# Key blocks share a turning bank, and the planner's prices change, in a two-layer hybrid attention backbone

## The chip, the cores and the metric

The kernel runs on one core of one Trainium2 chip. The metric is the device time of one execution in microseconds; the time before is the median of three runs. A profile is taken of one further execution; its span goes from the first to the last instruction that the profiler records.

The engines are named as in the profile: PE is TensorE, PEld its weight loads, DVE is VectorE, ACT is ScalarE, POOL is GpSimd, and SP is the queue that issues most of the DMAs.

## The reference

Two trunk layers work on 512 latent tokens and 256 context tokens with 1024 features each, in fp32. A layer is:

```python
mod = c_silu @ ada_w + ada_b            # shift, scale, gate; the same for the context from c_ctx
hx = rmsnorm(x, norm_w) * (1 + scale) + shift
px = split_cols(hx @ w_in)              # q, k, v of three mixers and a gate: 4608 columns
ya = global_gqa(...)                    # A: 8 heads, 2 kv heads, all 768 keys, normed q/k, rotary
yb = neighbourhood_attn(...)            # B: 8 heads, 8 x 16 window of keys with a bias, plus 256 context keys
yc = window_gqa(...)                    # C: 8 heads, 2 kv heads, keys within 128, sink logit, plus context keys
ux = concat([ya, yb, yc]) * silu(px[9])
x = x + gate * (ux @ w_out)
```

Context tokens go through the same weights and read only context keys; in the second layer they are needed as keys and values alone. The output is the final RMSNorm of the latent stream.

## The kernel before

**Numbers.** Every fp32 factor is split into a rounded part and a rest (`wh`/`wl`, `hh`/`hl`, `pth`/`ptl`, the two halves of `qt` and `kt`), both in the type fp32r. A projection is three matmuls (high x high, high x low, low x high); the split of weights costs one ACT copy (L242) and one DVE or POOL subtraction (L245) per 128 x 512 chunk.

**Stages.** The first stage (`p0`) loads x, norms it, makes the first modulation and h block by block, and accumulates the first projections (L416) as each block of h arrives. Then for each layer a stage of projections and attention (`p1`) and a stage of the output projection (`p2`, L505). In `p1` a list (`PLAN`) pairs the attention of one pair of heads with the projections of a later pair, so that TensorE has matmuls while DVE and ACT do the softmax. The last pair of heads (mixer C, pair 3) has no projections beside it; it runs beside the reloads of `u` (`uf`, L485) and the first output products.

**Modulation.** `ada` (L210) multiplies the two conditioning vectors (128 x 2, stationary) with 256 columns of `ada_w` in four column groups of the array at once, in exact fp32: eight products a job, in eight jobs of the first stage and eight in layer 0's `p1`. The row sums of the norms are exact products with a column of ones (`n == 2`). The modulation of layer 1 is mostly done as dot products on DVE (L151).

**Softmax and values.** A unit is one head of one mixer. `scores` puts the scores of a 128-query tile in a bank `Sbig`, DVE takes the maximum, ACT the exponential into `P`. `values` then goes over key blocks: for each it turns the 128 x 128 blocks of `P` of those query tiles that see it into a bank `T` of 512 columns (TensorE transposes, L1031; two such banks), `pt_copy` takes the bank out as `pth` (ACT, L778) and `ptl` (DVE, L1024), and `pv` (L1028) multiplies them with the values into `Obig`. Mixer B is `NearUnit` (16 of them in both layers), mixer C `BandUnit` (16), mixer A `GlobalUnit`, the context queries `CtxUnit`. In a `BandUnit` the blocks 4 and 5 (context) are seen by four tiles, 0 and 3 by two, 1 and 2 by three; in a `NearUnit` 4 and 5 by four, the others by two each.

**Rotary of C.** `rope_c` copies the projection to `tA`, swaps the halves of the heads by four DMAs on SP into `tB` (SBUF to SBUF, L958), and multiplies and adds on POOL (L959 to L961). K of C is then split by ACT (L979), POOL (L980) and copied by DVE (L981).

**The order.** The order of the instructions on each engine is not that of the code. `arrange` makes a `Step` of every instruction with a price (`cost`): the time it holds its engine (`busy`) and the time until its result is there (`last`; for a DMA `move`). `Graph` collects which step needs which, and how many buffers each tile has. `Graph.run` plays all engines and their DMAs forward by list scheduling with a rank; `Graph.back` derives a new rank from behind; after six turns the best of the plays, by its own forecast, is fixed as the order of every engine: PE, ACT, DVE, POOL and SP, whose queue holds the DMAs. The engines work in this order on the chip, each waiting for what its next instruction needs. A price thus changes no instruction, only where it stands.

The prices before, in ns: an exact product of 128 columns 108, any other exact product 230; an fp32r product columns/2.4 plus 12 to 13.5; a POOL operation 190 + 2.14 per element; a DMA lands 2550 plus bytes/395 after it starts, one after the other in one pipe whatever its queue and source.

Of the kernel before, what the change touches and what calls it, by code (L numbers as in the profile page):

```python
# [751 lines left out]
def mixers(tc, nc, l, last, p1, ps, const, env):  # L752
# [274 lines left out]
    def mul(*args, **kw):  # L1027
        return nc.tensor.matmul(*args, **kw)  # L1028

    def turn(*args, **kw):  # L1030
        return nc.tensor.transpose(*args, **kw)  # L1031

    def pv(O, v, pt, o, c0, n, first, final):

        for x in range(2):
            a = mul(O if c0 is None else O[:, c0:c0 + n], v, pt[x][:, o:o + n], start=first and x == 0,
                                 stop=final and x == 1, skip_group_check=True)

            if first and x == 0 and "last" in opv:
                after(a, opv["last"])  # L1040
            if final and x == 1:
                opv["last"] = a.ins.name
# [117 lines left out]
    class BandUnit(Unit):  # L1160
# [32 lines left out]

        def values(self):
            O = psO()
            for n, kb in enumerate((4, 5, 0, 1, 2, 3)):
                qs = [i for i in range(4) if kb in self.pos[i]]
                T = psT()
                for j, i in enumerate(qs):
                    o = self.pos[i][kb]  # L1200
                    turn(T[:, j * 128:(j + 1) * 128], self.P[i][:, o:o + 128], ident)
                k = len(qs) * 128
                pt = pt_copy(T, k)
                yield k / 1200
                pv(O, self.v(kb), pt, 0, qs[0] * 128, k, n == 0, n == 5)
                yield k / 1200
            o_out(O, self.OT(), self.h, 0, NT)

    class NearUnit(Unit):
# [36 lines left out]

        def values(self):
            O = psO()
            for n, kb in enumerate((4, 5, 1, 2, 3, 0)):
                qs = [i for i in range(4) if kb in self.PLAN[i][4]]  # L1250
                T = psT()
                for j, i in enumerate(qs):
                    o = self.PLAN[i][4][kb]
                    turn(T[:, j * 128:(j + 1) * 128], self.P[i][:, o:o + 128], ident)
                k = len(qs) * 128
                pt = pt_copy(T, k)
                yield k / 1200
                out = O[:, qs[0] * 128:qs[0] * 128 + k] if kb else O.rearrange("p (t c) -> p t c", t=4)[:, 0:4:3]
                pv(out, self.v(kb), pt, 0, None, k, n == 0, n == 5)
                yield k / 1200  # L1260
            o_out(O, self.OT(), self.h, 0, NT)

# [211 lines left out]
    prev = None  # L1474
# [24 lines left out]
    for pair, items, n_ada in PLAN:  # L1499
# [3 lines left out]
        if pair is not None:  # L1503
            kind, i = pair
            if kind == "B":
                Q, K = made["b", i]
                prev = units("B", i, Q, K, made["v", i // 2][i % 2], lambda i=i: made["g", i // 2][i % 2], bmb)
            else:
                Q, G = made[kind.lower(), i]
                K, V = made[kind.lower() + "kv", 0]  # L1510
                prev = units(kind, i, Q, K, V, G, bmc if kind == "C" else None)
# [6 lines left out]
        t = sum(time[k] for k, i in items)  # L1518
# [6 lines left out]
    prev = units("C", 3, Q, K, V, G, bmc)  # L1525
# [21 lines left out]
            xn1=8, rbl=2)  # L1547
POOLS = ("p0_", "p1_0_", "p2_0_", "p1_1_", "p2_1_")
BANKS = ("pj", "T", "Sbig", "Obig")
TO_PE, TO_OTHER, FIXED, RATE = 400.0, 150.0, 2550.0, 395.0  # L1550
ISSUE = dict(tB=580.0, R5=520.0, R2=520.0, wr=680.0)
WAIT = {"PE": 53.0, "POOL": 78.0, "ACT": 36.0, "DVE": 36.0, "SP": 30.0}
BEHIND = {"ACT": 112.0, "DVE": 85.0, "POOL": 45.0}
# [2 lines left out]
def stem(name):  # L1556
    return name.rsplit("_", 1)[0]
# [9 lines left out]
class Step:  # L1567


    def __init__(self, inst):  # L1570
        self.inst, self.name = inst, inst.name
        self.engine = ENGINES[str(inst.engine).split(".")[-1]]
        self.kind = type(inst).__name__
        self.dma = self.kind == "InstDMACopy"
        self.use = []
        for args, writes in ((inst.ins, 0), (inst.outs, 1)):
            for a in args:
                b = getattr(a, "bass_ap", None)
                if b is not None:
                    self.use.append((b.tensor, writes, tuple((int(p), int(q)) for p, q in a.ap), int(b.offset),  # L1580
                                     str(a.dtype).split(".")[-1]))
        self.cost()

    def cost(self):
        ins = [u for u in self.use if not u[1]]
        outs = [u for u in self.use if u[1]]
        n = max([size(u[2]) for u in ins + outs[:1]] or [0])
        bank = any(stem(u[0].name) in BANKS for u in ins)
        op = str(getattr(self.inst, "op", getattr(self.inst, "func", ""))).split(".")[-1]
        e = self.engine  # L1590
        self.plain, self.turn, self.switch = False, None, 0.0
        if self.dma:
            b = 4 * outs[0][2][0][1] * size(outs[0][2])
            self.busy = ISSUE.get(stem(outs[0][0].name).split("_")[0], 430.0)
            self.move = 3460.0 if stem(outs[0][0].name) == "bc" else b / RATE
        elif e == "PE":
            n = size(ins[0][2])
            exact = ins[0][4] == "float32"
            self.turn = outs[0][0].name if stem(ins[0][0].name) in ("ident", "identr") and n == 128 else None
            self.switch = 5.0 if exact else 86.0  # L1600
            self.busy = (108.0 if n == 128 else 230.0) if exact else n / 2.4 + (13.5 if n > 128 else 12.0)
            self.last = 272.0 if exact else n / 2.4 + 180.0
        else:
            if e == "ACT":
                d = 172.0 + 0.83 * n + (0 if bank else 35)
            elif e == "DVE":
                d = 156.0 + 0.52 * n if self.kind == "InstTensorCopy" and not bank else 152.0 + 1.06 * n
                self.plain = self.kind == "InstTensorTensor" and not bank and n >= 256
            elif op == "pow":
                d = 1000.0  # L1610
            elif self.kind == "InstTensorScalarPtr":
                d = 440.0 + 2.2 * n if n > 8 else 190.0
            else:
                d = 190.0 + 2.14 * n if n > 64 else 150.0
            self.busy = max(d - BEHIND[e], 20.0)
            self.last = d
            if e == "ACT" and op == "Exp" and n > 12:
                self.busy, self.last = d - 16, d + 91
# [18 lines left out]
class Graph:  # L1637
# [76 lines left out]
    def run(self, rank):  # L1714

        steps, n = self.steps, len(self.steps)
# [12 lines left out]
        for t, v in self.order.items():  # L1729
            if self.pool[t] is not None:  # L1730
                stage_left[self.pool[t]] += len(v)
        lanes, pipe = [], 0.0
        prev, done = None, 0

        def push(k):
            heapq.heappush(later[steps[k].engine], (ready[k], rank[k], k))
# [9 lines left out]
        while done < n:  # L1746
            t, e = min((max(free[e], -1.0 if now[e] else later[e][0][0]), e) for e in later if now[e] or later[e])
            free[e] = t = max(t, free[e])
            while later[e] and later[e][0][0] <= t:
                _, r, k = heapq.heappop(later[e])  # L1750
# [7 lines left out]
            r, k = heapq.heappop(now[e])  # L1758
            s = steps[k]
            need, wait = t, None  # L1760
            for name in self.opens[k]:
                tag = self.tag[name]
                p = self.pool[tag]
# [20 lines left out]
                wake(tag, t)  # L1784
            busy = s.busy
            if s.dma:
                pipe = fin = max(t + FIXED, pipe) + s.move
                lanes.append(fin)
            elif e == "PE":
                fin = t + s.last  # L1790
                if not s.turn and prev is not None and prev.turn:
                    busy += prev.switch
                    fin += prev.switch
                prev = s
            else:
                extra = 0.55 * min(free["POOL"] - t, s.last) if s.plain and free["POOL"] > t else 0.0
                fin = t + s.last + extra
                busy += extra
# [5 lines left out]
            for name in self.touch[k]:  # L1804
                uses[name] -= 1
                ends[name] = max(ends.get(name, 0.0), fin)
                if not uses[name]:
# [3 lines left out]
                    p = self.pool[tag]  # L1811
# [5 lines left out]
            for j in self.after[k]:  # L1817
                x = fin + self.gap(s, steps[j]) if self.before[j][k] else t
# [55 lines left out]

def arrange(tc, nc, needed):

    steps = [Step(i) for i in nc.cur_bb.bb.instructions
             if type(i).__name__ not in ("BassTilePoolBoundary", "InstRegisterMove")]
    tiles = {t.name: (t.tag, "DRAM" in str(t.space)) for t in tc.tiles}
    graph = Graph(steps, tiles, needed)  # L1880
    first = [(s.inst.bass_priority, k) for k, s in enumerate(steps)]
    rank, best = first, None
    for _ in range(CFG["turns"]):
        start, end, busy, streams = graph.run(rank)
        if best is None or max(end) < best[0]:
            best = max(end), streams
        at = graph.back(start, end, busy)
        rank = [(-t, k) for k, t in enumerate(at)]
    for ks in best[1].values():
        for a, b in zip(ks, ks[1:]):  # L1890
            tc.add_manual_dep(steps[b].inst, steps[a].name, mybir.DependencyInfo(mybir.DependencyClass.NoSync,
                                                                                mybir.DependencyReason.DATA),
                              reason="order")
# [98 lines left out]
```

## Time and profile before

| | |
|---|---|
| median of 3 runs | 1174.3 us (1171.54 to 1176.37) |
| the profiled execution | 1174.18 us |
| its span | 1172.4 us |
| mean granted clock of TensorE | 0.995 |
| DMA | 124.21 MB, mean 106 GB/s |
| copies L778 / L1024 | 312 each |

A row of the stretches view gives a stretch, its length, the busy time of each engine with the number of instructions, the granted clock, the DMA share and the rate. A row of groups gives line, engine, operation, output and inputs, shapes and count, then the busy time, the mean ns of one, and the idle time ahead of them with what ended it. A row of the timeline gives start and duration in us, and in brackets how long the engine had stood and what released it. A row of waits gives who waited for whom, us in total, times, longest. Matmuls are pipelined: the duration of one reaches over the start of the next, so that TensorE's pace is read from starts.

### The profile page before, as it was taken

The numbers are of one execution on the slowest core, as the hardware profiler recorded it, in microseconds if no ns is written. First come the engines' busy times: TensorE is split into PE (matmuls) and PEld (weight loads), VectorE is DVE, ScalarE is ACT, GpSimd is POOL, SyncE is SP. The second block draws the span as 40 slices with busy tenths as digits, with TensorE's granted clock in tenths as the row PEclk, the third lists the DMA queues.
The fourth block names the chain that finished last, engine by engine and source line by source line (L and its number), as shares of the span: only waits on it lengthen the run. The fifth ranks groups of instructions, "written<-read, shape, count | busy, mean of one in ns | idle before, by whom it ended". The sixth has DMA issues, their size and how long they took to land. (4 is left out here: it accounts for less than half of the span.)

```text
span 1172.4 us, 21741 instructions
## 1 busy us (share of the span) xinstructions
PE 1138.2 (97%) x8016; PEld 1031.2 (88%) x8016; DVE 764.4 (65%) x1548; ACT 699.5 (60%) x1581; POOL 405.6 (35%) x496
## 2 busy tenths in 40 slices
PE   5999999999999999999999999999999999999996
PEld 3798989998899898998888999988998989997885
DVE  5667666575456666667989755676665566667753
ACT  5446556565557667668733634555666677778641
POOL 2441111225436446366300030221245665556001
PEclk9999999999999999999999999999999999999998
DMA  9633223313222223113568542232232121123152
GB/s 350 220 93 102 87 70 95 102 55 112 82 69 86 82 67 97 59 37 104 161 235 282 159 141 86 69 118 84 82 95 68 62 66 55 55 66 106 37 171 72
DMA packets 60825, 124.21 MB, mean 106 GB/s; under 512 B 7216, under 2 KB 13488, under 8 KB 60720
## 3 DMA queue, kind: packets, MB, share of 16 engines
q1 hardware_dynamic: 56688, 114.58, 30.7%
q10 hardware_dynamic: 4032, 8.26, 1.8%
q8 instruction: 63, 1.03, 0.4%
q14 instruction: 42, 0.34, 0.1%
HBM read 109.05 MB, written 11.14 MB: 103 GB/s over the span
## 5 line engine op out<-in xcount | busy, mean ns | idle before, releaser
L1024 DVE TENSOR_TENSOR ptl<-T,pth 128x512 fp32r<-128x512 f32 (+2 forms) x312 | 181.4, 590 | 106.8 <-ACT pth L778 100.6
L778 ACT ACTIVATE pth<-T 128x512 fp32r<-128x512 f32 (+2 forms) x312 | 160.3, 521 | 96.1 <-PE T L1031 91.1
L329 PE MATMUL pj<-wh,hL 128*128 128x256 f32 x896 | 186.0, 286 | 0.0
L308 PE MATMUL pj<-hL,wh 128*128 128x512 f32 x544 | 181.4, 401 | 0.0
L1031 PE MATMUL T<-ident,P 128*128 128x128 f32 x1024 | 162.4, 274 | 5.4 <-DVE ptl L1024 4.3
L242 ACT ACTIVATE wh<-ws 128x512 fp32r<-128x512 f32 x192 | 119.7, 628 | 70.3 <-PE pj L308 18.6
L1028 PE MATMUL Sbig<-kt,qt 128*128 128x256 f32 (+1 forms) x864 | 160.7, 307 | 0.9 <-DVE negm L1240 0.8
L329 PEld LDWEIGHTS pj<-wh,hL 128*128 128x128 f32 x896 | 146.6, 190 | 1.3 <-issue 0.4
L1031 PEld LDWEIGHTS T<-ident,P 128*128 128x128 f32 x1024 | 121.4, 140 | 26.2 <-DVE ptl L1024 8.4
L1028 PEld LDWEIGHTS Sbig<-kt,qt 128*128 128x128 f32 x864 | 124.6, 190 | 8.8 <-DVE negm L1240 1.9
L1028 PE MATMUL Obig<-pth,vt 128*128 128x256 f32 (+2 forms) x432 | 129.2, 309 | 1.7 <-DVE OT L1047 1.6
L245 POOL TENSOR_TENSOR wl<-ws,wh 128x512 fp32r<-128x512 f32 x76 | 98.0, 1294 | 93.7 <-ACT wh L242 82.7
L1028 PE MATMUL Obig<-ptl,vt 128*128 128x256 f32 (+2 forms) x432 | 130.0, 315 | 0.2 <-DVE ptl L1024 0.2
L329 PE MATMUL pj<-wl,hL 128*128 128x256 f32 x448 | 127.7, 285 | 0.0
L245 DVE TENSOR_TENSOR wl<-ws,wh 128x512 fp32r<-128x512 f32 x116 | 82.6, 721 | 44.3 <-ACT wh L242 34.9
L308 PEld LDWEIGHTS pj<-hL,wh 128*128 128x128 f32 x544 | 97.7, 189 | 14.4 <-ACT wh L242 0.4
L308 PE MATMUL pj<-hL,wl 128*128 128x512 f32 x272 | 108.9, 400 | 0.1
L1028 PEld LDWEIGHTS Obig<-pth,vt 128*128 128x128 f32 x432 | 81.8, 189 | 7.5 <-DVE OT L1047 2.0
L329 PEld LDWEIGHTS pj<-wl,hL 128*128 128x128 f32 x448 | 85.2, 190 | 1.1
L1028 PEld LDWEIGHTS Obig<-ptl,vt 128*128 128x128 f32 x432 | 81.9, 189 | 3.5 <-DVE ptl L1024 0.4
L1413 POOL TENSOR_TENSOR bm<-wr,bm 128x192 f32<-128x192 f32 (+1 forms) x48 | 36.5, 788 | 136.8 <-DMA bm<-mskB_dram 46.7
L1133 DVE TENSOR_REDUCE negm<-Sbig 128x1 f32<-128x768 f32 x64 | 61.1, 955 | 28.2 <-ACT P L1135 14.8
(336 smaller groups left out, 2505.3 us busy)
## 6 DMA issues: line engine op xcount, KB each, us to landing
ws<-wf_dram SPq DMA_DIRECT2D x72, 256.0 KB, 3.0
ws<-wt_dram SPq DMA_DIRECT2D x72, 256.0 KB, 3.0
ada<-adaw_dram SPq DMA_DIRECT2D x32, 512.0 KB, 5.7
ws<-wo_dram SPq DMA_DIRECT2D x57, 256.0 KB, 2.9
bm<-mskB_dram SPq DMA_DIRECT2D x16, 576.0 KB, 3.4
dots<-adat_dram SPq DMA_DIRECT2D x16, 256.0 KB, 3.5
dw<-adat_dram SPq DMA_DIRECT2D x8, 512.0 KB, 6.9
u<-u ACTq DMA_DIRECT2D x9, 384.0 KB, 3.1
```

Of the source, the lines that this page charges most:

```text
L242: nc.scalar.activation(hi, src, AF.Copy)
L245: eng.tensor_sub(lo, src, hi.bitcast(F32))
L308: nc.tensor.matmul(p[:, 0:n], a[:, r, :], cols(b[kt], c0, n), start=(i == 0), stop=(i == 23))
L329: nc.tensor.matmul(p[:, t * 256:(t + 1) * 256], tok(a[kt], t2 + t), b[:, r, :], start=(i == 0), stop=(i == 23))
L778: nc.scalar.activation(out, src, AF.Copy)
L1024: nc.vector.tensor_sub(lo[:, 0:n], T[:, 0:n], hi[:, 0:n].bitcast(F32))
L1028: return nc.tensor.matmul(*args, **kw)
L1031: return nc.tensor.transpose(*args, **kw)
L1133: nc.vector.tensor_reduce(nm, S, axis=AX.X, op=OP.max, negate=True)
L1413: nc.gpsimd.tensor_add(b, src, b)
```

## The change

In `BandUnit.values` the key blocks 0 and 3 share one bank: their four turnings go into one `T`, one `pt_copy` of 512 columns takes it out, and two value products read its halves. In `NearUnit.values` blocks 1 and 3 share one, and 2 and 0. The order of the blocks changes accordingly (the last is 2 in a `BandUnit`, 0 in a `NearUnit`, as before for the latter).

In `Step.cost` and `Graph.run` the prices change. An exact product of 256 columns (modulation) is 57 ns, one of 2 columns (row sums) 112. Before 21 us all TensorE times are doubled. The third and later of a row of turnings in fp32r hold TensorE 20 ns longer. A DMA starts 2400 ns after its issue when it reads HBM and 1650 otherwise, moves 340 or 395 bytes per ns, follows the transfers of its own queue, is slowed by half the overlap with another queue, and lands 700 ns after its move.

```diff
@@ BandUnit
         def values(self):
             O = psO()
-            for n, kb in enumerate((4, 5, 0, 1, 2, 3)):
-                qs = [i for i in range(4) if kb in self.pos[i]]
+            for kbs in ((4,), (5,), (0, 3), (1,), (2,)):
                 T = psT()
-                for j, i in enumerate(qs):
+                jobs = [(kb, [i for i in range(4) if kb in self.pos[i]]) for kb in kbs]
+                for j, (kb, i) in enumerate((kb, i) for kb, qs in jobs for i in qs):
                     o = self.pos[i][kb]
                     turn(T[:, j * 128:(j + 1) * 128], self.P[i][:, o:o + 128], ident)
-                k = len(qs) * 128
+                k = 128 * sum(len(qs) for _, qs in jobs)
                 pt = pt_copy(T, k)
                 yield k / 1200
-                pv(O, self.v(kb), pt, 0, qs[0] * 128, k, n == 0, n == 5)
+                o = 0
+                for kb, qs in jobs:
+                    pv(O, self.v(kb), pt, o, qs[0] * 128, len(qs) * 128, kb == 4, kb == 2)
+                    o += len(qs) * 128
                 yield k / 1200
@@ NearUnit
-            for n, kb in enumerate((4, 5, 1, 2, 3, 0)):
+            for kbs in ((4,), (5,), (1, 3), (2, 0)):
...
@@ Step.cost
         if self.dma:
             b = 4 * outs[0][2][0][1] * size(outs[0][2])
-            self.busy = ISSUE.get(stem(outs[0][0].name).split("_")[0], 430.0)
-            self.move = 3460.0 if stem(outs[0][0].name) == "bc" else b / RATE
+            out = stem(outs[0][0].name).split("_")[0]
+            far = any(u[0].name not in tiles or tiles[u[0].name][1] for u in ins)
+            self.busy = ISSUE.get(out, 430.0)
+            self.fixed = 2400.0 if far else 1650.0
+            self.move = 3460.0 if out == "bc" else b / (340.0 if far else 395.0)
...
-            self.busy = (108.0 if n == 128 else 230.0) if exact else n / 2.4 + (13.5 if n > 128 else 12.0)
+            self.busy = {128: 108.0, 256: 57.0, 2: 112.0}[n] if exact else n / 2.4 + (13.5 if n > 128 else 12.0)
@@ Graph.run
             if s.dma:
-                pipe = fin = max(t + FIXED, pipe) + s.move
+                begin = max(t + s.fixed, ring.get(e, 0.0))
+                fin = begin + s.move
+                for x, (a, b) in data.items():
+                    if x != e:
+                        fin += 0.5 * max(0.0, min(b, fin) - max(a, begin))
+                ring[e], data[e] = fin, (fin - s.move, fin)
                 lanes.append(fin)
+                fin += TO_LAND
             elif e == "PE":
                 fin = t + s.last
                 if not s.turn and prev is not None and prev.turn:
                     busy += prev.switch
                     fin += prev.switch
+                row = row + 1 if s.turn else 0
+                if row > 2 and s.switch > 5:
+                    busy += 20
+                if t < SLOW:
+                    busy *= 2
+                    fin += s.last
```

Beside this, `TO_LAND` is 700, `SLOW` 21000, and `FIXED` (2550) and `RATE` (395) go.

More of the change, by code (lines that the diff above doesn't have):

```diff
@@ L1248, in values @@
             O = psO()
-            for n, kb in enumerate((4, 5, 1, 2, 3, 0)):
-                qs = [i for i in range(4) if kb in self.PLAN[i][4]]
+            for kbs in ((4,), (5,), (1, 3), (2, 0)):
                 T = psT()
-                for j, i in enumerate(qs):
+                jobs = [(kb, [i for i in range(4) if kb in self.PLAN[i][4]]) for kb in kbs]
+                for j, (kb, i) in enumerate((kb, i) for kb, qs in jobs for i in qs):
                     o = self.PLAN[i][4][kb]
                     turn(T[:, j * 128:(j + 1) * 128], self.P[i][:, o:o + 128], ident)
-                k = len(qs) * 128
+                k = 128 * sum(len(qs) for _, qs in jobs)
                 pt = pt_copy(T, k)
                 yield k / 1200
-                out = O[:, qs[0] * 128:qs[0] * 128 + k] if kb else O.rearrange("p (t c) -> p t c", t=4)[:, 0:4:3]
-                pv(out, self.v(kb), pt, 0, None, k, n == 0, n == 5)
+                o = 0
+                for kb, qs in jobs:
+                    n = len(qs) * 128
+                    out = O[:, qs[0] * 128:qs[0] * 128 + n] if kb else O.rearrange("p (t c) -> p t c", t=4)[:, 0:4:3]
+                    pv(out, self.v(kb), pt, o, None, n, kb == 4, kb == 0)
+                    o += n
                 yield k / 1200
@@ L1549 @@
 BANKS = ("pj", "T", "Sbig", "Obig")
-TO_PE, TO_OTHER, FIXED, RATE = 400.0, 150.0, 2550.0, 395.0
+TO_PE, TO_OTHER, TO_LAND = 400.0, 150.0, 700.0
+SLOW = 21000.0
 ISSUE = dict(tB=580.0, R5=520.0, R2=520.0, wr=680.0)
@@ L1567, with __init__ @@
 class Step:
-    def __init__(self, inst):
+    def __init__(self, inst, tiles):
         self.inst, self.name = inst, inst.name
@@ L1581, in __init__, with cost @@
                                      str(a.dtype).split(".")[-1]))
-        self.cost()
-    def cost(self):
+        self.cost(tiles)
+    def cost(self, tiles):
         ins = [u for u in self.use if not u[1]]
@@ L1731, in run @@
                 stage_left[self.pool[t]] += len(v)
-        lanes, pipe = [], 0.0
-        prev, done = None, 0
+        lanes, ring, data = [], {}, {}
+        prev, row, done = None, 0, 0
         def push(k):
@@ L1875, in arrange @@
 def arrange(tc, nc, needed):
-    steps = [Step(i) for i in nc.cur_bb.bb.instructions
+    tiles = {t.name: (t.tag, "DRAM" in str(t.space)) for t in tc.tiles}
+    steps = [Step(i, tiles) for i in nc.cur_bb.bb.instructions
              if type(i).__name__ not in ("BassTilePoolBoundary", "InstRegisterMove")]
-    tiles = {t.name: (t.tag, "DRAM" in str(t.space)) for t in tc.tiles}
     graph = Graph(steps, tiles, needed)
```

## The prediction

> **What bounds the kernel now.** I read the page's busy shares first, then the run cut into ten stretches, then the list of what TensorE waited for, and last the timeline around each long wait.
>
> ```profile
> span 1172.4 us, 21741 instructions
> PE 1138.2 (97%) x8016; PEld 1031.2 (88%) x8016; DVE 764.4 (65%) x1548; ACT 699.5 (60%) x1581; POOL 405.6 (35%) x496
> ```
>
> TensorE works in 97% of the span, so a change that leaves its instructions alone can only win what it idles, 34.2 us. Where that lies (columns: stretch, length, busy PE, PEld, DVE, ACT, POOL, granted clock, DMA share, GB/s):
>
> ```profile
> 0.00:11.45 11.45, 0.00 (x1) 0.00 (x1) 6.05 (x19) 6.42 (x10) 0.69 (x6) 1.00 0.83 281
> 11.45:60.00 48.55, 45.10 (x344) 32.20 (x345) 32.13 (x81) 25.71 (x62) 20.62 (x17) 1.00 0.76 278
> 60.00:280.00 220.00, 219.82 (x1657) 208.68 (x1657) 147.14 (x316) 127.47 (x310) 50.33 (x82) 1.00 0.28 86
> 280.00:300.00 20.00, 17.94 (x120) 15.36 (x119) 9.29 (x17) 10.53 (x21) 11.38 (x8) 0.91 0.31 103
> 300.00:560.00 260.00, 258.24 (x1920) 233.65 (x1919) 161.64 (x322) 175.13 (x409) 136.14 (x161) 1.00 0.25 79
> 560.00:600.00 40.00, 37.79 (x227) 32.27 (x226) 38.58 (x88) 25.03 (x59) 10.05 (x10) 1.00 0.57 176
> 600.00:1050.00 450.00, 448.87 (x3128) 414.51 (x3127) 297.63 (x586) 262.71 (x581) 147.92 (x185) 1.00 0.33 105
> 1050.00:1070.00 20.00, 18.09 (x103) 15.03 (x102) 14.07 (x22) 16.94 (x37) 13.85 (x14) 1.00 0.39 110
> 1150.00:1172.40 22.40, 12.32 (x96) 11.46 (x94) 6.25 (x12) 2.88 (x6) 4.86 (x7) 0.81 0.27 94
> ```
>
> Before 11.45 us TensorE has no data, and after 1150 us it sits in the chain of the last norm and the last stores: 21.5 us that no edit here touches. Between lie 3.45, 0.18, 2.06, 1.76, 2.21, 1.13 and 1.91 us, 12.7 in all. The even stretches (60 to 280 and 600 to 1050) lose 1.31 us in 670: a computed order can pack TensorE almost without holes. The holes stand elsewhere, and the list of waits names them (who, for whom, us, times, longest):
>
> ```profile
> PE T L1031 <- DVE ptl L1024: 4.3, 6, 1.4
> PE Sbig L364 <- POOL rstd L356: 1.3, 1, 1.3
> PE T L218 <- ACT adasb L214: 1.2, 1, 1.2
> PE pj L416 <- ACT wh L242: 0.7, 1, 0.7
> ```
>
> One hole costs more than its idle time. Around 291 us:
>
> ```profile
> 290.00:293.50 3.50, 1.70 (x12) 1.24 (x10) 2.00 (x5) 1.38 (x3) 3.42 (x2) 1.00 0.00 0
> 293.50:297.20 3.70, 3.44 (x16) 3.47 (x17) 2.63 (x7) 2.61 (x7) 0.59 (x1) 0.54 0.00 0
> ```
>
> After 3.5 us with TensorE busy for only 1.70, the next 3.7 us ran at a granted clock of 0.54, and 3.44 us of work at that clock is worth 1.86 at full: some 1.6 us lost beside the 2.06 of idle time, 3.7 for the place. The Trainium skill ("TensorE: Matmul & The Clock Gate", Part 1) has the clock fall after at least one idle window of about 3.4 us. This trace differs, since a half-busy stretch was enough; by the page the place would be worth its idle time alone, and the sum below would end some 1.3 us higher, at 1169.5.
>
> **The shared turnings.** The number and shapes of TensorE's turnings and value products stay: a BandUnit had groups of 512, 512, 256, 384, 384, 256 columns and gets 512, 512, 512, 384, 384; a NearUnit had 512, 512 and four of 256 and gets four of 512. What could change on TensorE is the number of switches from turning to matmul.
>
> ```profile
> 202.71 1.04 PE L1031 MATMUL T<-ident,P 128*128 128x128 f32 x8
> 203.50 0.36 PE L329 MATMUL pj<-wl,hL 128*128 128x256 f32 x1
> 203.70 0.40 PE L329 MATMUL pj<-wh,hL 128*128 128x256 f32 x2
> 205.49 0.38 PE L1031 MATMUL T<-ident,P 128*128 128x128 f32 x2
> 205.62 0.36 PE L329 MATMUL pj<-wh,hL 128*128 128x256 f32 x1
> 205.83 0.39 PE L1028 MATMUL Obig<-ptl,vt 128*128 128x512 f32 x1
> ```
>
> Eight turnings and one matmul take 203.70 - 202.71 = 0.99 us, two and one take 205.83 - 205.49 = 0.34. The difference is 0.65 for six turnings, 0.108 each, which leaves 0.12 for the matmul and nothing for the switch. So 48 fewer switches (16 NearUnits x 2, 16 BandUnits x 1) are worth 0 on TensorE. On the other engines each pair of 256 becomes one of 512:
>
> ```profile
> L1024 DVE TENSOR_TENSOR ptl<-T,pth 128x512 fp32r<-128x512 f32 x184 | 124.7, 686 | 63.7 <-ACT pth L778 59.7 <-PE Obig L1028 2.5
> L1024 DVE TENSOR_TENSOR ptl<-T,pth 128x256 fp32r<-128x256 f32 x96 | 39.7, 419 | 32.9 <-ACT pth L778 30.7 <-issue 1.9
> L778 ACT ACTIVATE pth<-T 128x512 fp32r<-128x512 f32 x184 | 109.0, 598 | 48.6 <-PE T L1031 45.6 <-DVE ptl L1024 1.1
> L778 ACT ACTIVATE pth<-T 128x256 fp32r<-128x256 f32 x96 | 36.2, 383 | 38.3 <-PE T L1031 36.3 <-DVE ptl L1024 0.9 <-PE Obig L1028 0.3
> ```
>
> DVE saves 2 x 419 - 686 = 152 ns and ACT 2 x 383 - 598 = 168 ns a pair, 7.3 and 8.1 us over 48. Neither engine is the bound, except that DVE is busy for 38.58 of 40 us between 560 and 600, where only a few pairs stand (under 0.5 us). Against it, the value products of a merged pair wait for 598 + 686 ns of copying in place of 383 + 419, 0.48 us more; four turnings now stand ahead of that copy instead of two. Other TensorE work hides this wherever there is any (60 to 280 us lost 0.18). Uncovered it would cost 0.48 for each of the six or so pairs at the two ends of the attention, 3 us at worst. I take 0 for gain and loss together.
>
> **The new prices.** They compute nothing, but `arrange` deals the order of every engine anew from them: all DMAs on SP's queue, POOL's bias fills and norms, each copy. Three prices bear on the holes.
>
> ```profile
> 12.39 1.03 PE L210 MATMUL T<-ada,silu_c 128*2 128x256 f32 x8
> 21.20 1.04 PE L210 MATMUL T<-ada,silu_c 128*2 128x256 f32 x16
> 313.87 1.04 PE L210 MATMUL pj<-ada,silu_c 128*2 128x256 f32 x16
> 314.85 0.73 PE L1028 MATMUL Sbig<-kt,qt 128*128 128x256 f32 x3
> ```
>
> *Modulation.* A job has eight products in the code (two halves, four groups), two records each in the trace. It takes 314.85 - 313.87 = 0.98 us. The old price is 8 x 230 = 1.84 us, the new one 8 x 57 = 0.46. Priced too dear, a job puts TensorE 0.86 us ahead of its plan, so it reaches work whose inputs are not there; priced too cheap, TensorE comes 0.52 us late and the inputs wait, which costs nothing. The eight jobs of layer 0 lie between 283 and 495 us. That stretch and its surroundings idle 2.06 + 1.76 us, whereas 600 to 1050, without such jobs, idles 1.13 in a longer time.
>
> ```profile
> 289.61 4.49 POOL L980 TENSOR_TENSOR kt<-tR,kt 64x768 fp32r<-64x768 f32 x2 [0.96 <-ACT kt L979]
> 291.47 0.95 DVE L981 CAST kt<-kt 64x1536 fp32r<-64x1536 f32 x1 [5.15 <-POOL kt L980]
> 292.93 0.38 PE L1028 MATMUL Obig<-pth,vt 128*128 128x256 f32 x1 [1.61 <-DVE OT L1047]
> ```
>
> The worst hole has both causes: DVE stood 5.15 us for POOL, whose two subtractions took 4.49 us where the planner has 2 x 1.83, so 0.8 us of lateness; and the job at 283 us put TensorE 0.86 ahead. Together they make the 1.61. The change mends only the second.
>
> *Half clock.* Eight records took 1.03 us at 12.39, sixteen 1.04 at 21.20: TensorE ran at half speed until about 21 us. The old plan does not know it; the new one doubles PE's times there, which should bring the chain to the first h (norm, modulation, weight copy) ahead of modulation for later blocks. The holes that it can mend are the 1.2, 1.3 and 0.7 of the list.
>
> *DMA.* Columns end in KB and the median us to landing:
>
> ```profile
> ws<-wf_dram SPq DMA_DIRECT2D x72, 256.0 KB, 3.0
> uf<-u SPq DMA_DIRECT2D x9, 384.0 KB, 3.2
> tB<-tA SPq DMA_DIRECT2D x40, 64.0 KB, 2.0
> 1061.01 0.63 ACT L477 ACTIVATE hL<-uf 128x512 fp32r<-128x512 f32 x1 [1.57 <-DMA uf<-u]
> 1063.61 0.44 PE L1031 MATMUL T<-ident,P 128*128 128x128 f32 x2 [1.44 <-DVE ptl L1024]
> ```
>
> For `ws` the old price is 2.55 + 262144/395 ns = 3.21 us, the new 2.40 + 262144/340 ns + 0.70 = 3.87; for `uf` 3.55 becomes 4.26; for `tB` 2.72 becomes 2.52. So loads from HBM are now planned dear and land early, on average. That matters at 1061 us, where ACT stood 1.57 us for a reload with the copy of a turning queued behind it, and TensorE then idled 1.44.
>
> **The sum.** The profiled execution took 1174.18 us, the span and 1.8 beside it, 0.1 under the median of 1174.3. My takings are estimates between nothing and the whole hole:
> - 280 to 300: bounds 0 and -3.7; I take -3.0, since the clock recovers as soon as a part of the hole is filled;
> - 300 to 560: 0 and -1.8; half, -0.9;
> - 560 to 600: 0 and -2.2; -0.8, as the DVE there stays nearly full;
> - 1050 to 1070: 0 and -1.9; -1.4, the wait for the reload;
> - 11.45 to 60: 0 and -3.5; -1.5, as POOL's 1.3 is no matter of order;
> - new holes where nothing stood: +1.5. The even stretches lose 0.2 us in 100, which is 0.9 over the other 470 us, and one more line speaks of what no price knows:
>
> ```profile
> 568.53 1.81 DVE L1099 TENSOR_SCALAR negm<-negm,negsink 128x2 f32<-128x2 f32 x1
> ```
>
> a two-column operation that took 1.81 us, so a hold of over 1.5 us may fall anywhere in a new order.
>
> Together -6.1, so 1168.2 us.
>
> **The rivals.** *All holes go:* 12.7 us and 1.6 of clock, 1160 us; more likely 1160 to 1165. For it speaks how even the other stretches are; against it that POOL's times and the DVE holds keep their wrong prices. *The holes are dealt again:* as many stand elsewhere, 1172 to 1177. For it: the new modulation price misses by 0.52 us the other way, so the plan still does not fit, and most holes (4.3 us behind `ptl`) come from DVE and POOL times that are not repriced. *Slower:* dear loads are issued early, and SP works in order. A load that stands on SP until its buffer is free (three of `ws`, three of `gt`) holds the four swaps of a rotary projection (`tB`) queued behind it, so the rotated K or Q comes late, as at 291 us, at 3.7 us a place. There are ten such projections (40 swaps). Two places eat the 6.1 saved; four cost 14.8, and 14.8 - 6.1 = 8.7 slower is 1183 us. Against it: from 60 to 1050 us the DMA share is 0.25 to 0.33, so loads seldom queue for the wires. *The change doesn't do what it says:* the modulation price is at half of the measured time; this helps TensorE, by the argument above, and so has no chance of its own.
>
> **How the numbers follow.** This kernel's measurement tells about 0.5%, 5.9 us, from no change. The forecast, 1165 to 1171, gets 0.50, half of it beyond 0.5%; all holes gone 0.18; dealt again 0.20; slower by over 0.5% 0.12. Faster is 0.25 + 0.18 = 0.43, same 0.25 + 0.20 = 0.45. The range leaves out the ends of the two outer cases, and runs from 1161 to 1177.
>
> **What would show it.** Right: 264 copies at L1024 instead of 312, with none of 256 columns in place of 96; about the same PE busy time and instruction count; no stretch at half clock near 290 us; PE idle between 11.45 and 1150 us down from 12.7 to some 8; the wait for `uf` at the end of layer 1 gone. Wrong: the same idle sum at other places, or PE waiting for rotated K and Q with `tB` late on SP. A drop in PE's busy time of more than 3 us would mean that order costs TensorE something inside its busy time, which I have at nothing.

## The result, and the profile after

| | before | after |
|---|---|---|
| median | 1173.06 us (1170.75 to 1176.37, 7 runs) | 1166.70 us (1164.97 to 1168.59, 7 runs) |
| ratio | | 0.9945, 95% interval 0.9929 to 0.9961 |
| profiled execution, span | 1174.18, 1172.4 us | 1167.82, 1166.0 us |

The change makes the kernel 6.4 us faster; the prediction had 6.1. The first two lines of the page after:

```profile
span 1166.0 us, 21590 instructions
PE 1137.1 (98%) x8016; PEld 1032.5 (89%) x8016; DVE 758.8 (65%) x1500; ACT 691.8 (59%) x1533; POOL 404.5 (35%) x496
```

TensorE runs the same 8016 instructions. Its busy time falls by 1.1 us, and its idle time from 34.2 to 28.9. DVE and ACT lose 48 instructions each, and 5.6 and 7.7 us. In the groups by shape the copies of 256 columns are gone, and 232 of 512 columns stand where 184 stood:

```profile
L1024 DVE TENSOR_TENSOR ptl<-T,pth 128x512 fp32r<-128x512 f32 x232 | 157.7, 687 | 105.0 <-ACT pth L778 103.5
```

The stretches, cut as for the kernel before (stretch, length, busy PE, PEld, DVE, ACT, POOL, granted clock, DMA share, GB/s):

```profile
11.45:60.00 48.55, 47.57 (x350) 33.90 (x350) 30.88 (x86) 25.47 (x61) 19.67 (x17) 1.00 0.68 255
60.00:280.00 220.00, 218.57 (x1642) 207.39 (x1643) 145.59 (x301) 123.61 (x291) 51.10 (x81) 1.00 0.30 92
280.00:300.00 20.00, 19.37 (x142) 16.48 (x140) 10.84 (x20) 12.44 (x27) 13.29 (x9) 1.00 0.36 115
300.00:560.00 260.00, 259.00 (x1940) 236.18 (x1939) 162.54 (x325) 175.58 (x406) 139.53 (x166) 1.00 0.25 80
560.00:600.00 40.00, 37.15 (x207) 31.32 (x206) 36.86 (x79) 22.31 (x51) 4.91 (x3) 0.96 0.45 144
600.00:1050.00 450.00, 449.47 (x3138) 415.41 (x3138) 299.89 (x567) 263.79 (x569) 147.92 (x189) 1.00 0.34 107
1050.00:1070.00 20.00, 19.73 (x121) 17.03 (x120) 15.08 (x21) 17.00 (x35) 16.76 (x13) 1.00 0.30 90
```

Length less busy PE gives the idle time of TensorE: 0.98, 1.43, 0.63, 1.00, 2.85, 0.53 and 0.27 us, 7.7 in all against 12.7. The hole near 291 us and the one at 1062 are gone. The stretch from 560 to 600 has become worse, 2.85 against 2.21, and the half clock that stood at 293 us now stands there (0.96). In the list of waits the first line is the wait for the first norm, 11.4 us before and 11.5 after; behind it stand:

```profile
PE pj L364 <- POOL rstd L356: 1.9, 1, 1.9
PE Obig L1028 <- DVE ptl L1024: 1.8, 2, 1.6
PE T L1031 <- DVE ptl L1024: 1.5, 4, 0.6
PE T L329 <- DVE wl L245: 1.0, 1, 1.0
```

The 1.9 us stand in the chain at the end in both kernels. The turnings' wait for `ptl` fell from 4.3 us to 1.5, and the waits of 1.6 (`OT`), 1.3 (`Sbig` for `rstd`) and 1.2 us (`adasb`) are gone.

Idle time alone can mislead where the clock changes. So I also counted TensorE's work: each matmul at its pace from start to start (0.12 us for 256 columns of fp32r, 0.23 for 512, 0.109 for a turning, and so on), 1118.5 us in every kernel here, and read when the same sum is reached. The paces are rounded, so a line is good to about half a us.

| work done, us | before | after | difference | since the line above |
|---|---|---|---|---|
| 70 | 93.45 | 93.52 | +0.1 | +0.1 |
| 250 | 274.25 | 274.78 | +0.5 | +0.5 |
| 280 | 308.43 | 306.24 | -2.2 | -2.7 |
| 500 | 534.47 | 529.26 | -5.2 | -3.0 |
| 540 | 577.55 | 574.92 | -2.6 | +2.6 |
| 1000 | 1040.56 | 1036.74 | -3.8 | -1.2 |
| 1070 | 1113.55 | 1107.52 | -6.0 | -2.2 |

The first stage gained nothing, although TensorE idles 2.5 us less there. Eight records of modulation took 1.03 us at 20.95 and 0.61 at 25.11 in the kernel after, so half clock held until after 21 us; in the kernel before sixteen took 1.04 at 21.20, which is full clock already. The trace's record of the granted clock has full clock from 24.95 us after the change and from 20.60 before it.

```profile
20.95 1.03 PE L210 MATMUL T<-ada,silu_c 128*2 128x256 f32 x8
25.11 0.61 PE L210 MATMUL T<-ada,silu_c 128*2 128x256 f32 x8
```

The new hole between 560 and 600 us, in the timeline after:

```profile
566.49 2.41 DVE L151 CUSTOM_DVE_ANT_0 junk<-dots,sm 128x512 bf16<-128x512 f32 x1
566.50 1.85 POOL L478 TENSOR_TENSOR kt<-uf,kt 128x768 fp32r<-128x768 f32 x1
...
568.83 0.68 DVE L1024 TENSOR_TENSOR ptl<-T,pth 128x512 fp32r<-128x512 f32 x1
569.43 0.74 DVE L151 CUSTOM_DVE_ANT_0 junk<-dots,sm 128x512 bf16<-128x512 f32 x1
569.56 0.50 PE L1028 MATMUL Obig<-ptl,vt 128*128 128x512 f32 x1 [1.57 <-DVE ptl L1024]
```

The same dot product took 2.41 us at 566.49 and 0.74 at 569.43. The long one began together with a POOL subtraction and came free 0.5 us after that one's end (568.35). I call this a hold. The copy that TensorE needed, 0.68 us long and with its input in a bank, stood behind it. The Trainium skill ("SBUF — State Buffer", the part on SBUF's two separate sides) says that VectorE and GpSimd share one pair of ports as an exclusive lock, which a DVE operation with two SBUF inputs needs when GpSimd reads SBUF too, and which is kept for a whole instruction. This trace agrees, 2.41 us against 0.74.

### The profile page after: what moved, and what is told of

Same layout as the page of the kernel before. It is cut to its first block, busy times and chain, and to the rows that moved or that the text cites. A ratio compares the mean times of both kernels' runs of the same rounds, so it can differ in the third digit from the quotient of the medians.

```text
span 1166.0 us, 21590 instructions
## 1 busy us (share of the span) xinstructions
PE 1137.1 (98%) x8016; PEld 1032.5 (89%) x8016; DVE 758.8 (65%) x1500; ACT 691.8 (59%) x1533; POOL 404.5 (35%) x496
## 3 DMA queue, kind: packets, MB, share of 16 engines
q8 instruction: 63, 1.03, 0.4%
## 5 line engine op out<-in xcount | busy, mean ns | idle before, releaser
L1024 DVE TENSOR_TENSOR ptl<-T,pth 128x512 fp32r<-128x512 f32 (+1 forms) x264 | 174.3, 671 | 109.0 <-ACT pth L778 107.3
L778 ACT ACTIVATE pth<-T 128x512 fp32r<-128x512 f32 (+1 forms) x264 | 152.8, 587 | 95.6 <-PE T L1031 92.1
L1031 PE MATMUL T<-ident,P 128*128 128x128 f32 x1024 | 154.4, 274 | 2.5 <-DVE ptl L1024 1.5
```

Of the source, the lines that this page charges most:

```text
L778: nc.scalar.activation(out, src, AF.Copy)
L1024: nc.vector.tensor_sub(lo[:, 0:n], T[:, 0:n], hi[:, 0:n].bitcast(F32))
```

## The experiments

Each kernel is compared with the kernel before on the same chip. A ratio under 1 is faster than before.

| kernel | prices | groups | ratio | 95% interval | median us |
|---|---|---|---|---|---|
| the change | new | merged | 0.9945 | 0.9929 to 0.9961 | 1166.70 |
| e1_merge_only | old | merged | 0.9946 | 0.9934 to 0.9959 | 1166.49 |
| e2_prices_only | new | old | 0.9929 | 0.9915 to 0.9943 | 1164.48 |
| e3_products_only | products new | old | 0.9974 | 0.9964 to 0.9985 | 1170.19 |
| e4_dma_only | DMA new | old | 0.9987 | 0.9978 to 0.9996 | 1170.88 |
| e5_half_clock_only | half clock new | old | 1.0024 | 1.0013 to 1.0034 | 1175.62 |
| e6_neutral_before | old, turning 107 ns | old | 0.9935 | 0.9922 to 0.9947 | 1165.29 |
| e12_neutral_before2 | old, turning 109 ns | old | 0.9968 | 0.9957 to 0.9980 | 1169.15 |
| e9_neutral_after | new, turning 107 ns | merged | 0.9943 | 0.9931 to 0.9955 | 1166.31 |
| e7_true_product | new, products true | merged | 0.9944 | 0.9931 to 0.9957 | 1165.80 |
| e8_hold | new, holds | merged | 0.9840 | 0.9826 to 0.9855 | 1153.64 |
| e11_hold_neutral | new, holds, turning 107 | merged | 0.9881 | 0.9868 to 0.9893 | 1158.62 |
| e10_hold_before | old, holds | old | 0.9922 | 0.9909 to 0.9934 | 1163.41 |

My theory was that of the prediction: each price mends the holes that its error had made. The rival: any edit deals the order anew, holes fall elsewhere, and the kernel before was a poor deal.

**Each part alone.** e1 is the kernel before with the two `values` functions of the change; e2 is the change with the two functions of before.

> The shared turnings with the old prices. Theory 'each price mends its own holes': TensorE has no gain from the merge and the holes of before stay, so a ratio of 0.998 to 1.002 to the kernel before, with the half-clock stretch near 290 us still there. Rival 'any new order is a new deal': the order is dealt anew here as well (264 copies in place of 312), so it may land anywhere from 0.994 to 1.003, and the hole near 290 us need not be there. Rival 'the merge does it': 0.994 to 0.996.

> All new prices without the shared turnings. Theory 'each price mends its own holes': the whole gain, 0.993 to 0.996. Rival 'the merge does it': 0.999 to 1.001. Rival 'new deal': anywhere from 0.994 to 1.003.

My theory had 0.998 to 1.002 for e1, and falls there: each half alone brings as much as the whole, within the intervals. Of the holes of before, e1 kept the one near 291 us (TensorE waits 1.54 us for `OT` at 291.44) and lost the half clock behind it. So the halves do not add up, and "the merge does nothing" cannot be read from e1, nor "the merge does it", since e2 has the gain without it.

e3, e4 and e5 take one price each into the kernel before:

```diff
# e3
-            self.busy = (108.0 if n == 128 else 230.0) if exact else ...
+            self.busy = {128: 108.0, 256: 57.0, 2: 112.0}[n] if exact else ...
# e4: the DMA lines of the change alone
# e5, in Graph.run
+                if t < 21000.0:
+                    busy *= 2
+                    fin += s.last
```

> The kernel before with the prices of modulation and row-sum products alone changed (57 and 112 ns). Theory 'each price mends its own holes': the holes of 280 to 560 us, some 5 us (0.995 to 0.997), and PE idle there under 1.7 us against 3.8; the late hole near 1062 us stays. Rival 'new deal': the idle time of 280 to 560 us is no smaller than in an order dealt anew for no reason (the neutral kernel of this call).

> The kernel before with the new DMA prices alone (2400 or 1650 ns, a pipe for each queue, 700 ns to land). Theory 'each price mends its own holes': the late hole at 1062 us, behind a reload, goes (idle of 1050 to 1070 us under 0.5 against 1.9), the one at 291 us stays: 0.997 to 0.999. Rival 'new deal': holes elsewhere, 0.994 to 1.003.

> The kernel before with TensorE's times doubled up to 21 us of the plan, nothing else. The changed kernel gained nothing in the first 70 us by equal work done, so theory 'each price mends its own holes' expects 0.999 to 1.001 with the first matmul of h nearer to 20 than to 23 us and the half clock lasting longer. Rival 'new deal': later stretches move too, 0.995 to 1.003.

Multiplied, the three give 0.9974 x 0.9987 x 1.0024 = 0.9985, where all prices together gave 0.9929; the fourth price, 20 ns on rows of turnings in fp32r, had no run of its own. e3 came out just slower than expected. Its idle time from 280 to 560 us fell only from 3.8 to 2.5 us, not under 1.7, and a half-clock stretch appeared near 566 us. e4 has the ratio that I expected, not the mechanism: from 1050 to 1070 us it idles 0.66 us and not under 0.5, the hole at 291 that was to stay has given way to a wait of 1.27 us at 293.6 for another input, and a half clock stands at 571 us. e5 refutes the half clock as a gain: its first product of h begins at 28.4 us, where I had expected it nearer to 20 than to 23. Its stretches:

```profile
11.45:60.00 48.55, 43.26 (x313) 30.36 (x310) 34.44 (x82) 26.95 (x62) 17.83 (x15) 1.00 0.78 280
280.00:300.00 20.00, 18.10 (x120) 15.49 (x119) 10.05 (x19) 10.96 (x22) 10.74 (x7) 0.91 0.34 112
```

TensorE idles 5.29 us in the first stage in place of 3.45, and 70 us of work are done at 96.36 us in place of 93.45, 2.9 late. The hole near 291 us is still there: this edit left the later order nearly as it was, and that hole came with the order.

**A price that corrects nothing.** e6 and e12 are the kernel before with the exact turning at 107 and 109 ns, e9 is the change with 107; the trace's pace is 108 to 109.

```diff
-            self.busy = (108.0 if n == 128 else 230.0) if exact else ...
+            self.busy = (107.0 if n == 128 else 230.0) if exact else ...
```

> The kernel before with one price changed by 1 ns (exact turning 107 in place of 108), which corrects nothing and only deals the order anew. Theory 'each price mends its own holes': within 0.2% of the kernel before, with holes of about 12 us in total between 11 and 1150 us. Rival 'new deal': it moves by 0.3% or more either way, and the holes stand elsewhere.

> The kernel before with the exact turning at 109 in place of 108 ns, a second deal of the old prices. If the kernel before was a poor deal among its like, this one too is faster, 0.991 to 0.998; if the first neutral deal was a lucky one, 0.998 to 1.004.

> The changed kernel with the exact turning priced at 107 in place of 108 ns, a new deal of the changed kernel that corrects nothing. Theory 'new deal' (the neutral deal of the kernel before came out at 0.9935, as fast as the change): a few us either side of the changed kernel, 0.990 to 1.000 of before. Rival 'the new prices hold the holes down': it stays within 0.2% of the changed kernel, 0.993 to 0.996.

One nanosecond makes the kernel before as fast as the change does. In e6 the modulation costs what it did, 230 ns, and yet:

```profile
280.00:300.00 20.00, 20.00 (x138) 16.65 (x137) 11.08 (x22) 12.17 (x26) 11.86 (x8) 1.00 0.34 111
560.00:600.00 40.00, 38.75 (x222) 31.81 (x220) 36.31 (x80) 21.02 (x49) 5.42 (x3) 1.00 0.60 196
```

No hole and no half clock from 280 to 300 us, with the wrong price that I had blamed for them. What is different there can be followed back to the four swaps of K's rotary. In the kernel before:

```profile
L958 SPq DMA_DIRECT2D tB<-tA x4: 582/588/591, 277.1 to 279.0; - x4
DMA to landing us min/median/max: 2.0/2.0/4.5
278.66 0.33 ACTq L1341 DMA_DIRECT2D u<-u  x1
283.63 1.27 POOL L960 TENSOR_TENSOR tB<-tB,tabx 128x512 f32<-128x512 f32 x1 [2.99 <-DMA tB<-tA]
```

and in e6:

```profile
L958 SPq DMA_DIRECT2D tB<-tA x4: 582/585/590, 275.6 to 277.5; - x4
DMA to landing us min/median/max: 2.0/2.0/2.1
277.98 0.33 ACTq L1341 DMA_DIRECT2D u<-u  x1
279.79 1.30 POOL L960 TENSOR_TENSOR tB<-tB,tabx 128x512 f32<-128x512 f32 x1 [1.18 <-DMA tB<-tA]
```

Before, the last swap was issued 0.35 us after a store of `u` (384 KB) on ACT's queue and took 4.5 us to land. POOL stood 2.99 us for it, and behind POOL's chain came the copy of K, `OT` and TensorE's 1.61. In e6 all four swaps were issued ahead of the store and landed within 2.1 us. With 2.1 in place of 4.5 POOL could have begun some 2.4 us earlier, more than the hole; this is an estimate, as no run changes that alone. It fits the other traces: e1, e5 and e12 have late swaps too (4.3 us or more) and the same hole, 1.46 to 1.84 us. In e3 the swap is late (4.3), but the copy of K stands further behind in DVE's queue, and the longest wait there is 0.87 us. In the seven kernels with the new DMA price, by which transfers of two queues slow each other, no swap there takes over 3.7 us; in the seven without it five have one that does. So a price may have mended this hole after all, though not the one I named; e6 and e10 do without it.

The old prices give 1, 0.9935 and 0.9968 in three deals, mean 0.9968, with 0.65% from end to end, more than the whole change. The new prices with merged groups give 0.9945, 0.9943 and, with the products as measured, 0.9944.

> The changed kernel with the modulation product at 112 ns and the row-sum product at 224, which is what a whole product of two records takes in the trace. Theory 'priced too cheap costs nothing': no difference to the changed kernel, 0.993 to 0.996 of before. Rival 'only the true price helps': a further 1 to 2 us in 280 to 560 us, 0.991 to 0.994. Rival 'new deal': anything from 0.990 to 1.000.

So e7 shows no cost of a product priced at half of its time, as expected; one below the scatter of the deals would not be seen. It also adds a third deal. The three lie within 0.02%, as the rival in e9's expectation had it ('the new prices hold the holes down'). Whether the new prices are worth the 0.24% between the means, or nothing, three deals of each kind can't tell, as the old ones lie 0.65% apart. That stays open.

**The hold.** The planner before and after adds to a DVE subtraction 0.55 of the time that POOL still works, up to the subtraction's own. The traces show other DVE operations held until POOL's operation is done. In the kernel before, the two-column operation at 568.53 us began beside a POOL subtraction of 568.08 to 570.32 and ended at 570.34; free of POOL it takes 0.21. Copies out of a bank are not held: none of the 312 took over 0.69 us.

```profile
L1024 DVE TENSOR_TENSOR ptl<-T,pth x312: 360/678/693, 99.1 to 1111.5; 128x512 fp32r<-128x512 f32 x92, 128x256 fp32r<-128x256 f32 x48, 128x384 fp32r<-128x384 f32 x16
```

The hold works both ways: the copy of K at 291.47 us took its usual 0.95, and the POOL subtraction that came up behind it took 2.58 in place of 1.83. e8 prices the hold of DVE for every DVE operation that reads no bank:

```diff
-                self.plain = self.kind == "InstTensorTensor" and not bank and n >= 256
+                self.plain = not bank
...
-                extra = 0.55 * min(free["POOL"] - t, s.last) if s.plain and free["POOL"] > t else 0.0
+                extra = 0.9 * (free["POOL"] - t) if s.plain and free["POOL"] > t else 0.0
```

> The changed kernel whose planner also knows that a DVE operation without a bank that starts while POOL works is held (0.9 of what POOL has left is added to it; before 0.55 and for large subtractions alone). If the holds make the remaining holes (566 us: DVE 2.41 us in place of 0.74, TensorE idle 1.57 and the clock halved for 3.4 us), the stretch 560 to 600 us gains 2 to 3 us and the whole is at 0.990 to 0.993 of before. Rival 'new deal': as likely slower as faster than the changed kernel.

> The changed kernel with the price of the DVE holds, dealt anew by 107 in place of 108 ns. If the price of the holds is the cause, 0.982 to 0.988; if the first was a lucky deal of many, 0.990 to 0.997.

> The kernel before with the price of the DVE holds alone; old prices and old groups otherwise. If the hold is what the order lacked, most of the 1.6% is here: 0.984 to 0.989. If it needs the new prices beside it, 0.990 to 0.996; if the 1.6% was a lucky deal, 0.993 to 1.002.

All three are faster than each of the ten other edits (the fastest is e2, 0.9929; e10's interval overlaps it, those of e8 and e11 do not). A lucky deal is thus no likely cause for e8, though the deals differ here too, by 0.41% between e8 and e11. e8 gained more than its expectation had, and e11 came out just beside the range for the hold as the cause. On the old prices the hold brings less than I expected from it as the main cause (0.9922), so it works better beside the other edits, or e10 was a poorer deal. By the ratios the price of the hold is worth some 12 us in e8 (against the change), 7 in e11 (against e9) and 5 in e10 (against the mean of the three old deals). e8 is the best version of all (0.9840/0.9945 = 0.9895 of the change). Its page and stretches:

```profile
PE 1127.0 (98%) x8016; PEld 1028.8 (89%) x8016; DVE 762.0 (66%) x1500; ACT 690.6 (60%) x1533; POOL 405.8 (35%) x496
```

```profile
280.00:300.00 20.00, 20.00 (x139) 17.27 (x138) 12.71 (x20) 10.65 (x23) 8.22 (x6) 1.00 0.21 66
300.00:560.00 260.00, 259.65 (x1963) 238.69 (x1962) 170.78 (x337) 182.98 (x424) 144.61 (x169) 1.00 0.28 88
560.00:600.00 40.00, 39.96 (x233) 34.59 (x232) 33.52 (x76) 16.96 (x36) 0.00 (x0) 1.00 0.64 214
```

DVE is not busy for less (762.0 us against 758.8), so it is not held for less in all, but at places where TensorE doesn't wait for what is behind: no wait for `ptl` is left in TensorE's list (3.9 us after the change). TensorE idles 0.04 us between 560 and 600 in place of 2.85; POOL's last subtraction of that part, at 566.50 after the change, stands at 557.7. The place that began all this, in e8:

```profile
282.60 3.75 POOL L980 TENSOR_TENSOR kt<-tR,kt 64x768 fp32r<-64x768 f32 x2 [0.95 <-ACT kt L979]
...
284.40 0.42 DVE L1047 TENSOR_TENSOR OT<-Obig,otmp 64x256 f32<-64x256 f32 x1
284.85 2.31 DVE L981 CAST kt<-kt 64x1536 fp32r<-64x1536 f32 x1
```

The copy of K is held for longer than in the kernel before (2.31 us; there it took 0.95 once DVE had stood 5.15 for its input). But `OT`, which frees the bank for TensorE, now stands ahead of it and not behind. Of the gain, 3.3 us are there when 70 us of work are done (90.24 us against 93.52 after the change), about 7 at 500 and 13.3 at 540 (561.67 against 574.92). The first 3.3 are not shown to come from the hold: full clock is on record from 16.66 us in e8, from 24.95 after the change. TensorE's busy time is lower by 10.1 us, its idle time by 4.6: a wait lies in part under the modelled end of the matmul ahead of it and counts as busy, and so does work at half clock. What each has of the 10.1 was not measured.

## Why the prediction was right, and where it was wrong

- **What bounds the kernel** held: TensorE's instructions stayed, and only its waits moved. But more can be won than its idle time: the prediction had nothing inside the busy time, which fell by 1.1 us here and by 11.2 in e8 against the kernel before.
- **The merge at 0 on TensorE**: no run speaks against it, none shows it alone, because each edit deals the order anew. The 152 and 168 ns of a pair were 7.3 and 8.1 us over 48; DVE and ACT fell by 5.6 and 7.7.
- **280 to 300, -3.0**: measured -2.7 by equal work, near it. **300 to 560, -0.9**: -3.0 up to 500 us of work. The step that failed is the cause: "the job at 283 us put TensorE 0.86 ahead ... The change mends only the second". e6 lost the hole without mending it; what stood at its start was a swap that took 4.5 us to land where its like take 2.0. The other half of the working, POOL 0.8 us late by its subtractions, was misread: the first took 1.83 us, as priced, and DVE waited for that one alone; the second took 2.58 because DVE's copy ran. In the new hole at 566 us DVE stood at POOL too, not for a result but in the middle of an operation, again with work for TensorE behind it in its queue. The prediction saw such a hold (568.53 us, 1.81 us) and set it aside as "what no price knows"; e8 shows that a price can know it.
- **560 to 600, -0.8**: +2.6, the wrong sign; a hold and a half clock fell there.
- **11.45 to 60, -1.5**: +0.1, since half clock lasted longer. The 1.3 us for POOL's `rstd`, called no matter of order, went all the same. e5 shows the price of half clock alone to cost 2.9 us.
- **1050 to 1070, -1.4**: -2.2; that it was the price of DMA is not shown: the stretch idles 0.66 us in e4, with that price alone, but 0.60 in e6, with the old one.
- **New holes, +1.5**: +0.5 in the stretch from 60 to 280, and a gain of 1.2 from 600 to 1050.
- **The rival *slower*** was read against a DMA share of 0.25 to 0.33 from 60 to 1050 us; the prediction's own row from 560 to 600 has 0.57. Its mechanism, late `tB`, was at work in the kernel before.

What the prediction named as signs came: 264 copies, no half clock near 290 us, idle time of 7.7 for "some 8". They could not tell the two theories apart. No half clock near 290 us is in part luck as well: e1 and e12 have the hole there and not the clock, for a reason shown at the end. That terms so far off add up to 6.0 us, where 6.1 was forecast, is luck. Where TensorE loses time was read rightly, what makes the holes go was not. The rival "the holes are dealt again" is enough to explain the result, and I gave it the wrong outcome, as many holes as before: the kernel before had more than its like.

## What to carry to other kernels

Before an edit to a planned order is credited with a gain, deal the same order anew by an edit that means nothing: here 1 ns moved the time by as much as the whole change. A hole is worth tracing to the instruction that stands ahead of the late one in its engine's queue; here a DVE operation held by POOL, whose pricing was worth 5 to 12 us in three kernels, and a DMA issued just after one of another queue.

## What the runs showed of the hardware

Between the first stage and the chain at the end the clock falls for 3.41 us at a time, and it goes by the 3.41 us right before. The lengths on record between two changes of the clock are multiples of 3.413 us, so each trace can be cut into such windows from a change on. Two windows in a row, in the kernel before near 290 and near 1062 us, then in e5, the change and e12:

```profile
290.25:293.66 3.41, 1.45 (x11) 1.02 (x9) 2.11 (x5) 1.13 (x3) 3.33 (x2) 1.00 0.00 0
293.66:297.08 3.42, 3.32 (x15) 3.35 (x16) 2.51 (x5) 2.54 (x6) 0.43 (x1) 0.50 0.00 0
1061.66:1065.07 3.41, 1.97 (x12) 1.52 (x11) 3.40 (x5) 2.25 (x6) 1.53 (x2) 1.00 0.45 152
1065.07:1068.48 3.41, 3.41 (x23) 3.01 (x21) 2.56 (x5) 3.36 (x8) 3.34 (x4) 1.00 0.29 88
```

```profile
292.92:296.33 3.41, 1.64 (x12) 1.20 (x10) 2.11 (x5) 1.16 (x3) 3.34 (x2) 1.00 0.00 0
296.33:299.75 3.42, 3.29 (x15) 3.32 (x16) 2.52 (x5) 2.53 (x6) 0.47 (x1) 0.50 0.00 0
```

```profile
567.67:571.08 3.41, 1.63 (x10) 1.04 (x9) 3.41 (x8) 1.86 (x5) 0.68 (x1) 1.00 0.22 79
571.08:574.50 3.42, 3.42 (x13) 3.18 (x12) 2.58 (x6) 0.56 (x2) 0.00 (x0) 0.50 0.24 81
```

```profile
564.92:568.33 3.41, 1.69 (x8) 1.04 (x6) 3.41 (x3) 1.32 (x3) 3.10 (x2) 1.00 0.76 293
568.33:571.75 3.42, 2.97 (x19) 2.78 (x20) 3.42 (x9) 2.35 (x8) 0.00 (x0) 1.00 0.26 71
```

Busy for 1.45, 1.63 or 1.64 us of a window, TensorE ran the next at half clock; busy for 1.69 or 1.97, it did not. So about half a window of idling is enough, here some 1.75 us, and it may be made of several waits. In all fourteen traces, cut like this from 30 to 1100 us, five windows have TensorE busy for under 1.65 us, and half clock follows these five and no other. The page "TensorE: Matmul & The Clock Gate" of the Trainium skill (Part 1) asks for one idle window of about 3.4 us; its length agrees with these stretches, the need for a whole idle one does not. A window at half clock costs up to 1.7 us beside the idle time (an estimate, half of 3.41), so 1.8 us of waiting in one window can be twice as dear as 1.6. Where the edges fall decides too: e1 and e12 have the hole near 291 us, but no window with so little work. It changes from one execution to the next: in the 47 of the kernel before that ran beside the experiments the mean clock lies between 0.992 and 0.997; the 12 at 0.997 took 1171.9 us in the mean, the nine at 0.994 or less 1174.7.

In the first stage busy time is not all that counts. In e2 TensorE was busy for 2.40 us of a window, 1.1 of them with row sums and modulation, and the next window ran at half clock all the same; in the kernel before, a window with 2.31 us was followed by full clock, although it held such products too:

```profile
16.52:19.93 3.41, 2.40 (x23) 1.29 (x25) 3.12 (x9) 2.45 (x6) 0.00 (x0) 1.00 1.00 389
19.93:23.35 3.42, 3.42 (x16) 2.20 (x14) 1.86 (x6) 2.06 (x5) 0.70 (x1) 0.50 1.03 417
```

```profile
20.60:24.01 3.41, 2.31 (x22) 1.13 (x22) 3.06 (x11) 2.85 (x8) 1.48 (x1) 1.00 1.04 406
24.01:27.42 3.41, 2.49 (x16) 2.14 (x17) 2.15 (x6) 1.82 (x5) 3.33 (x3) 1.00 1.03 408
```

What counts there beside busy time stays open.
